# Two subtractions per tile move from VectorE to GpSimd, and six inner tiles change from eight to seven block products

## The chip, the cores and the metric

The kernel runs on one core of a Trainium2 chip. The metric is the device time of one execution in microseconds (us); the times below are those of separate runs, and one further execution was profiled. In the profile PE is TensorE (matmuls), PEld its weight loads, DVE is VectorE, ACT is ScalarE, POOL is GpSimd, SP is SyncE, which here only issues transfers.

## The reference, cut to what matters

A trunk of two layers works on 512 frames of 1024 channels. Each layer has a mixer (layer 0 a recurrent one, layer 1 chunked attention), and behind it a channel mixer, which the change is about:

```
def conv_glu(h, w_in, conv_w, conv_b, w_out):
    gate, val = jnp.split(h @ w_in, 2, axis=-1)          # 1024 -> 2 x 2816
    gp = jnp.pad(gate, ((0, 0), (CONV_W - 1, 0), (0, 0)))
    conv = conv_b + sum(conv_w[j] * gp[:, j:j + seq] for j in range(CONV_W))
    return (jax.nn.gelu(conv, approximate=False) * val) @ w_out
```

The 2816 inner channels are 22 tiles of 128. For each tile a gate and a value are projected from 1024 inputs; the gate is convolved over three frames, goes through a GELU and multiplies the value.

## The kernel before, in words

**Split operands.** TensorE works here in a format with a shorter mantissa than float32 (fp32r). Each operand is therefore split into a high part (a cast, made on ScalarE) and a low part (the number less its high part, a subtraction made on VectorE), and each product is three matmuls: high by high, high by low, low by high. `split_w` (lines 172 and 178) does this for weight tiles of 128x1024, `split_to` (lines 218 and 219) for other operands, the result of each inner tile among them.

**Eights and sevens.** The function `ffn` makes the 22 inner tiles one after the other. A tile called an *eight* (`eight`) is computed plainly: two weight tiles, 2 x 8 x 3 = 48 matmuls on 512 columns. A tile called a *seven* (`seven`) treats gate and value, two halves of the inputs and two halves of the frames as a 2x2 by 2x2 block product and forms it from seven block products in place of eight, as Strassen and Winograd do: 7 x 4 x 3 = 84 matmuls on 256 columns. For this it needs sums and differences of the weight blocks, made by `operands`. Gate weights are loaded into `rg`, and a second transfer, issued by GpSimd (line 442), adds their one half onto the other while it moves. Value weights are loaded into a `wraw` buffer (line 443). VectorE forms one difference in `rg` (line 446) and two in the value tile (lines 448 and 449). Four operands come out: `wv` (the value weights as loaded), `w1`, `wy`, `wx`, each split into high and low. `SEVEN` says which tiles are sevens: of 4 to 20 all but 8, 13 and 18, so 14 sevens and 8 eights in a layer. Tiles 0 to 3 are eights, since sums of the inputs are still made then, and so is 21.

**Order.** The seven's products stand on TensorE's queue as P1 (`wv`), then P6 (`wy`) and P7 (`wx`) of the tile before, and then P2 (`w1`), P3 (`wy`), P4 (`wv`), P5 (`wx`). The result of a tile goes through `gated`: line 397 (ACT), 398 and 399 (DVE), 400 (the GELU, ACT), 401 (the product with the value, DVE), and then its split, a cast on ACT and a subtraction on DVE, into tile j of the inner result (`r1h`/`r1l` or `r2h`/`r2l` for tiles 0 to 7, `f3h`/`f3l` for the others). That low part is read only by the projection back to 1024 channels, behind the last inner tile. In this projection `both` also uses `operands`, three times in layer 0 and twice in layer 1.

**Buffers.** `rg` and `wraw` have two buffers each, `whi` and `wlo` three, `w1` and `wx` one, temporaries six. Each engine works through its queue in order, so an instruction that waits holds up all behind it on that engine; the queues are written in the order that the scheduler gives them at build time.

Of the kernel before, what the change touches and what calls it, by code (L numbers as in the profile page):

```python
# [13 lines left out]
ALU = mybir.AluOpType  # L14
# [98 lines left out]
def trunk_kernel(ctx, tc, A, out):  # L113
    nc = tc.nc
    PE, V, SC, GP = nc.tensor, nc.vector, nc.scalar, nc.gpsimd
# [25 lines left out]
    def Vc(name, i):  # L141
        return vec[:, VOFF[name][0] + i:VOFF[name][0] + i + 1]
# [20 lines left out]
    def tmp(dt=F32, shape=(P, S)):  # L163
        return banks["tmp"].tile(list(shape), dt, name="tmp", tag="tmp")
# [4 lines left out]
    def split_w(raw, n, src=None):  # L169
        hi = wp.tile([P, 1024], F32R, name="whi", tag="whi")  # L170
        lo = wp.tile([P, 1024], F32R, name="wlo", tag="wlo")
        SC.copy(hi[:, :n], raw)  # L172
        if src is not None:

            SC.activation(lo[:, :n], raw, AF.Copy, scale=-1.0)
            GP.dma_start(lo[:, :n], src, accum_op=ALU.add)
        else:
            V.tensor_tensor(lo[:, :n], raw, hi[:, :n], op=ALU.subtract)  # L178
        return hi, lo
# [37 lines left out]
    def split_to(h_, l_, src):  # L217
        SC.copy(h_, src)  # L218
        V.tensor_tensor(l_, src, h_, op=ALU.subtract)  # L219
# [124 lines left out]
            V.tensor_tensor(xT[:, m], xT[:, m], ps[:], op=ALU.add)  # L344
            norm_tile(xT[:, m], m, gain, h_, l_)

    SEVEN = [j for j in range(4, 21) if j % 5 != 3]
    HT = (slice(0, 256), slice(256, 512))

    def ffn(l, hp, ih, il, h_, l_, xT, after, last=None):  # L350
# [5 lines left out]
        def hid(j):  # L356
            return (h_[:, j], l_[:, j]) if j < 8 else (f3h[:, j - 8], f3l[:, j - 8])
# [21 lines left out]
        def sums(k):  # L379
            u, w = tmp(), tmp()  # L380
            for t_, q in ((u, k), (w, k + 4)):
                nc.sync.dma_start(t_[:], xd[q])
                SC.activation(t_[:], t_[:], AF.Copy, scale=Vc(f"ln2_{l}", q))
            four(k, u, w)
# [10 lines left out]
        def gated(j, g, v):  # L395
            c = tmp()
            SC.activation(c[:], g[:], AF.Identity, scale=Vc(f"cw2_{l}", j), bias=Vc(f"cb_{l}", j))
            V.scalar_tensor_tensor(c[:, 1:S], g[:, 0:S - 1], Vc(f"cw1_{l}", j), c[:, 1:S], op0=ALU.mult, op1=ALU.add)
            V.scalar_tensor_tensor(c[:, 2:S], g[:, 0:S - 2], Vc(f"cw0_{l}", j), c[:, 2:S], op0=ALU.mult, op1=ALU.add)
            SC.activation(c[:], c[:], AF.Gelu)  # L400
            V.tensor_tensor(c[:], v, c[:], op=ALU.mult)
            split_to(*hid(j), c[:])

        def eight(j):
            wg = load_w(A["ffn_in"][l, j, 0])
            wv = load_w(A["ffn_in"][l, j, 1])
            pg = ps_f()
            n = 0
            for _ in dense(pg[:], [(wg, K8)], act):
                n += 1  # L410
                if n == 2:
                    yield
            pv = ps_f()
            run(dense(pv[:], [(wv, K8)], act))
            g = tmp()
            V.tensor_tensor(g[:], pg[:], rho[:], op=ALU.mult)
            gated(j, g, pv[:])
# [12 lines left out]
        def own(name, n):  # L430
            return tuple(hp.tile([P, n], F32R, name=name + q, tag=name + q) for q in "hl")

        def split2(w, raw):
            split_to(w[0][:], w[1][:], raw)
            return w

        def operands(src_g, src_v):
            rv = wp.tile([P, 1024], F32, name="wraw", tag="wraw", bufs=2)
            rg = hp.tile([P, 1024], F32, name="rg", tag="rg", bufs=2)
            one, two = slice(0, 512), slice(512, 1024)  # L440
            nc.sync.dma_start(rg[:], src_g)
            GP.dma_start(rg[:, one], src_g[:, two], accum_op=ALU.add)
            nc.sync.dma_start(rv[:], src_v)
            wv = split_w(rv[:], 1024)
            w1 = split2(own("w1", 512), rg[:, one])
            V.tensor_tensor(rg[:, one], rg[:, one], rv[:, one], op=ALU.subtract)
            wy = split_w(rg[:], 1024)
            V.tensor_tensor(rv[:, one], rg[:, two], rg[:, one], op=ALU.subtract)
            V.tensor_tensor(rv[:, two], rv[:, two], rg[:, one], op=ALU.subtract)  # L449
            wx = split2(own("wx", 1024), rv[:])  # L450
            return wv, w1, wy, wx

        def seven(j):
            wv, w1, wy, wx = operands(A["ffn_in"][l, j, 0], A["ffn_in"][l, j, 1])
            b, c = ps_d((P, 256)), ps_f((P, 256))
            v, g = tmp(), tmp()
            prod(b[:], wv, 0, B(0, 0))
            SC.copy(v[:, HT[0]], b[:])
            yield
            prod(c[:], w1, 0, T(1))  # L460
            prod(b[:], wy, 0, T(2), False)
            SC.copy(v[:, HT[1]], b[:])
            a = ps_f((P, 256))
            prod(a[:], wv, 512, B(1, 0))
            V.tensor_tensor(v[:, HT[0]], a[:], v[:, HT[0]], op=ALU.add)
            prod(b[:], wx, 0, T(3), False)
            SC.copy(g[:, HT[1]], b[:])
            V.tensor_tensor(g[:, HT[1]], c[:], g[:, HT[1]], op=ALU.add)
            V.tensor_tensor(g[:, HT[1]], g[:, HT[1]], rho[:, HT[1]], op=ALU.mult)
            yield  # L470
            prod(b[:], wy, 512, T(4), False)
            V.tensor_tensor(g[:, HT[0]], b[:], rho[:, HT[0]], op=ALU.mult)
            prod(c[:], wx, 512, B(1, 1), False)
            V.tensor_tensor(v[:, HT[1]], c[:], v[:, HT[1]], op=ALU.add)
            gated(j, g, v[:])
# [5 lines left out]
        for j in range(NFF):  # L481
            t = (seven if j in SEVEN else eight)(j)
            next(t)
            if rest is not None:
                run(rest)
                rest = None
            if j in SEVEN:
                next(t)
# [3 lines left out]
            if j < 2:  # L492
                sums(2 * j)
                sums(2 * j + 1)
            if j == SEVEN[-1] + 1:
                xT = mid.tile([P, KD, S], F32, name="xT", tag="xT")
# [31 lines left out]
        def both(m):  # L528
            full = [A["ffn_out"][l, m + u] for u in range(2)]
            u0 = pieces(m, ((8, 7), (15, 7)))  # L530
            wv, w1, wy, wx = operands(full[1][:, :1024], full[0][:, :1024])
            yield
            d0 = ps_d()
            run(dense(d0[:], u0, hid))
            b, c = ps_f((P, 256)), ps_f((P, 256))
            s0, s1 = tmp(), tmp()
            prod(b[:], wv, 0, H(0, 0))
            SC.copy(s0[:, HT[0]], b[:])
            prod(c[:], w1, 0, T(1))
            prod(b[:], wy, 0, T(2), False)  # L540
            SC.copy(s0[:, HT[1]], b[:])
            V.tensor_tensor(s0[:, HT[1]], c[:], s0[:, HT[1]], op=ALU.add)
            prod(d0[:, HT[0]], wv, 512, H(1, 0), False)
            prod(b[:], wx, 0, T(3), False)
            SC.copy(s1[:, HT[1]], b[:])
            V.tensor_tensor(s1[:, HT[1]], c[:], s1[:, HT[1]], op=ALU.add)
            prod(b[:], wy, 512, T(4), False)
            SC.copy(s1[:, HT[0]], b[:])
            prod(d0[:, HT[1]], wx, 512, H(1, 1), False)
            u1 = pieces(m + 1, ((8, 7), (15, 7)))  # L550
            yield
            arrive(m, d0, s0)
            d1 = ps_d()
            run(dense(d1[:], u1, hid))
            arrive(m + 1, d1, s1)
# [995 lines left out]
```

## Time and profile before

| | |
|---|---|
| time, median of 3 runs | 1330.07 us (1328.38 to 1333.38) |
| the profiled execution: its time, its span | 1332.23 us, 1330.4 us |
| mean granted TensorE clock | 0.994 |
| busy in the span: PE, DVE, ACT, POOL | 97%, 76%, 54%, 5% |
| inner tiles of layer 0, of layer 1 (about) | 394 to 640 us, 969 to 1215 us |
| the projection behind them, layer 0, layer 1 | 640 to 740 us, 1215 us to the end |

The two stretches of inner tiles are a little over a third of the span. A row of the timeline gives start, duration, engine, line, operation and operands; since an engine begins an instruction while the one before it still writes its last results, the step from start to start is what one instruction takes of a full queue, and the duration is a little longer. In a row of the windows view, busy time and count of instructions stand for each engine in a stretch of time.

### The profile page before, as it was taken

The numbers are of one execution on the slowest core, as the hardware profiler recorded it, in microseconds if no ns is written. First come the engines' busy times: TensorE is split into PE (matmuls) and PEld (weight loads), VectorE is DVE, ScalarE is ACT, GpSimd is POOL, SyncE is SP. The second block draws the span as 40 slices with busy tenths as digits, with TensorE's granted clock in tenths as the row PEclk, the third lists the DMA queues.
The fourth block names the chain that finished last, engine by engine and source line by source line (L and its number), as shares of the span: only waits on it lengthen the run. The fifth ranks groups of instructions, "written<-read, shape, count | busy, mean of one in ns | idle before, by whom it ended". The sixth has DMA issues, their size and how long they took to land.

```text
span 1330.4 us, 24187 instructions
## 1 busy us (share of the span) xinstructions
PE 1293.9 (97%) x9472; PEld 1109.8 (83%) x9472; DVE 1013.8 (76%) x2143; ACT 718.9 (54%) x1236; POOL 67.6 (5%) x110
## 2 busy tenths in 40 slices
PE   7999999999999999999999999999999999999997
PEld 5787777776778999999888878786789999998887
DVE  8886889788468889998756776748678998987644
ACT  6555465555446656655334476657465655553431
POOL 0000000000010000001000000000100000010000
PEclk9998999999999999999999999999999999999999
DMA  5265544554264345355332322222643444453232
GB/s 213 94 178 115 112 101 110 114 127 119 81 205 143 103 128 147 99 135 176 87 108 78 131 88 88 95 95 88 190 166 102 115 126 123 131 167 109 83 87 77
DMA packets 72561, 160.88 MB, mean 121 GB/s; under 512 B 25984, under 2 KB 28288, under 8 KB 72448
## 3 DMA queue, kind: packets, MB, share of 16 engines
q1 hardware_dynamic: 62400, 132.34, 31.8%
q0 software_dynamic: 10048, 27.01, 10.0%
q8 instruction: 74, 1.21, 0.4%
q14 instruction: 39, 0.32, 0.1%
HBM read 148.31 MB, written 11.01 MB: 120 GB/s over the span
## 4 chain that ended last, share of the span: by engine, by line
PE 82%; DVE 10%; ACT 3%; DMA 3%; issue 2%; SPq 0%; DVEq 0%; ACTq 0%; POOLq 0%
PE psd L201 9%; PE psd L202 9%; PE psd L206 9%; PE psd L424 4%; PE psd L427 4%; PE psd L425 4%; PE psf L201 4%; PE psf L202 4%; PE psf L206 4%; PE psf L424 4%; PE psf L427 4%; PE psf L425 4%; DVE Xu L875 2%; DVE Xs L877 1%; PE pss L1328 1%
## 5 line engine op out<-in xcount | busy, mean ns | idle before, releaser
L172 ACT CAST whi<-wraw 128x1024 fp32r<-128x1024 f32 (+1 forms) x169 | 173.6, 1028 | 188.0 <-DMA wraw<-in_ffn_out_dram 44.3
L178 DVE TENSOR_TENSOR wlo<-wraw,whi 128x1024 fp32r<-128x1024 f32 (+1 forms) x150 | 178.8, 1192 | 79.9 <-ACT whi L172 37.7
L201 PE MATMUL psd<-r1h,whi 128*128 128x512 f32 x270 | 109.0, 404 | 0.9 <-DVE xT L344 0.9
L202 PE MATMUL psd<-r1l,whi 128*128 128x512 f32 x270 | 106.9, 396 | 0.0
L201 PE MATMUL psd<-f3h,whi 128*128 128x512 f32 (+1 forms) x238 | 88.8, 377 | 0.0
L202 PE MATMUL psd<-f3l,whi 128*128 128x512 f32 (+1 forms) x238 | 88.7, 377 | 0.0
L206 PE MATMUL psd<-r1h,wlo 128*128 128x512 f32 x270 | 74.1, 405 | 0.0
L201 PE MATMUL psd<-r2h,whi 128*128 128x512 f32 (+1 forms) x168 | 64.6, 389 | 0.8 <-ACT r2h L1335 0.7
L202 PE MATMUL psd<-r2l,whi 128*128 128x512 f32 (+1 forms) x168 | 63.9, 384 | 0.8 <-DVE r2l L219 0.8
L201 PEld LDWEIGHTS psd<-r1h,whi 128*128 128x128 f32 x270 | 50.8, 188 | 12.4 <-issue 1.8
L202 PEld LDWEIGHTS psd<-r1l,whi 128*128 128x128 f32 x270 | 51.0, 189 | 9.7 <-issue 0.3
L206 PEld LDWEIGHTS psd<-r1h,wlo 128*128 128x128 f32 x270 | 49.6, 191 | 10.6 <-issue 0.7
L424 PE MATMUL psd<-xh,whi 128*128 128x256 f32 x224 | 56.3, 284 | 0.0
L206 PE MATMUL psd<-f3h,wlo 128*128 128x512 f32 (+1 forms) x238 | 53.7, 377 | 0.0
L202 PEld LDWEIGHTS psd<-f3l,whi 128*128 128x128 f32 x238 | 44.8, 188 | 8.0
L201 PEld LDWEIGHTS psd<-f3h,whi 128*128 128x128 f32 x238 | 44.8, 188 | 8.0
L201 PE MATMUL psf<-r1h,whi 128*128 128x512 f32 x128 | 50.1, 391 | 0.0
L201 PE MATMUL psf<-r2h,whi 128*128 128x512 f32 x128 | 50.1, 391 | 0.0
L202 PE MATMUL psf<-r2l,whi 128*128 128x512 f32 x128 | 50.0, 390 | 0.0
L202 PE MATMUL psf<-r1l,whi 128*128 128x512 f32 x128 | 49.9, 390 | 0.0
L206 PEld LDWEIGHTS psd<-f3h,wlo 128*128 128x128 f32 x238 | 42.9, 188 | 8.2
L218 ACT CAST wxh<-wraw 128x1024 fp32r<-128x1024 f32 x33 | 34.4, 1044 | 20.2 <-DVE wraw L449 17.5
(538 smaller groups left out, 3757.9 us busy)
## 6 DMA issues: line engine op xcount, KB each, us to landing
wraw<-in_ffn_in_dram SPq DMA_DIRECT2D x60, 512.0 KB, 3.9
rg<-in_ffn_in_dram SPq DMA_DIRECT2D x28, 512.0 KB, 3.5
wraw<-in_ffn_out_dram SPq DMA_DIRECT2D x32, 448.0 KB, 3.4
wraw<-in_wA_dram SPq DMA_DIRECT2D x20, 512.0 KB, 4.0
wraw<-in_w_out_dram SPq DMA_DIRECT2D x16, 512.0 KB, 3.9
wlo<-in_wA_dram POOLq DMA_DIRECT2D x15, 512.0 KB, 7.7
rg<-in_ffn_in_dram POOLq DMA_DIRECT2D x28, 256.0 KB, 5.2
wraw<-in_ffn_out_dram SPq DMA_DIRECT2D x11, 512.0 KB, 3.6
```

Source lines behind the costliest of these rows:

```text
L172: SC.copy(hi[:, :n], raw)
L178: V.tensor_tensor(lo[:, :n], raw, hi[:, :n], op=ALU.subtract)
L201: PE.matmul(ps, wh[:, j * P:(j + 1) * P], ah, start=start and n == 0, stop=False)
L202: PE.matmul(ps, wh[:, j * P:(j + 1) * P], al, start=False, stop=False)
L206: PE.matmul(ps, wl[:, j * P:(j + 1) * P], act(k)[0], start=False, stop=stop and n == len(ks) - 1)
L218: SC.copy(h_, src)
L424: PE.matmul(ps, wh[:, ws], ah, start=start and k == 0, stop=False, skip_group_check=not start)
L425: PE.matmul(ps, wh[:, ws], al, start=False, stop=False, skip_group_check=not start)
L427: PE.matmul(ps, wl[:, o + k * P:o + k * P + P], a(k)[0], start=False, stop=k == 3, skip_group_check=not start)
L875: V.tensor_tensor(uv, L1.rearrange("p i o -> p o i").to_broadcast([P, k, n]), X[:, 0:k, q:q + 1].to_broadcast([P, k, n]), op=ALU.mult)
L877: V.tensor_tensor(X[:, 0:k, q + 1:], X[:, 0:k, q + 1:], uv, op=ALU.add)
L1328: PE.matmul(pso[HS[hh], kt * P:], vS[i // 2][:, kt, (i % 2 * 2 + hh) * 64:(i % 2 * 2 + hh + 1) * 64], pts[hh][:, kt, kt * P:], start=kt == ...
```

## The change

`SEVEN` becomes all tiles from 4 to 20: tiles 8, 13 and 18 of each layer turn from eights into sevens. The low part of every inner tile's result is subtracted on GpSimd, not on VectorE, and so is the second difference in the value tile of `operands`.

```diff
-    SEVEN = [j for j in range(4, 21) if j % 5 != 3]
+    SEVEN = list(range(4, 21))
...
         def gated(j, g, v):
...
             V.tensor_tensor(c[:], v, c[:], op=ALU.mult)
-            split_to(*hid(j), c[:])
+            SC.copy(hid(j)[0], c[:])
+            GP.tensor_tensor(hid(j)[1], c[:], hid(j)[0], op=ALU.subtract)
...
         def operands(src_g, src_v):
...
             V.tensor_tensor(rv[:, one], rg[:, two], rg[:, one], op=ALU.subtract)
-            V.tensor_tensor(rv[:, two], rv[:, two], rg[:, one], op=ALU.subtract)
+            GP.tensor_tensor(rv[:, two], rv[:, two], rg[:, one], op=ALU.subtract)
             wx = split2(own("wx", 1024), rv[:])
```

The changed file has one line more from line 403 on, so lines 442, 446, 448 and 449 are 443, 447, 449 and 450 there. The first place to look at is GpSimd's queue among the inner tiles of layer 0. Before, it holds the adding transfers alone, one for each seven:

```order
L442 DMA rg_5919<-in_ffn_in_dram 128x512
L442 DMA rg_6014<-in_ffn_in_dram 128x512
L442 DMA rg_6143<-in_ffn_in_dram 128x512
L442 DMA rg_6272<-in_ffn_in_dram 128x512
L442 DMA rg_6507<-in_ffn_in_dram 128x512
```

In the changed kernel it reads so (`rg_6200` belongs to tile 11, `rg_6329` to 12, `rg_6458` to 13, `rg_6587` to 14; `tmp_6008`, `tmp_6137`, `tmp_6266` are the results of tiles 8, 9 and 10):

```order
L403 TENSOR_TENSOR f3l_4966<-tmp_6008,f3h_4965 128x512
L443 DMA rg_6329<-in_ffn_in_dram 128x512
L450 TENSOR_TENSOR wraw_6199<-wraw_6199,rg_6200 128x512
L403 TENSOR_TENSOR f3l_4966<-tmp_6137,f3h_4965 128x512
L443 DMA rg_6458<-in_ffn_in_dram 128x512
L450 TENSOR_TENSOR wraw_6328<-wraw_6328,rg_6329 128x512
L403 TENSOR_TENSOR f3l_4966<-tmp_6266,f3h_4965 128x512
L443 DMA rg_6587<-in_ffn_in_dram 128x512
```

So each tile now has the difference for tile n, the low part of the result of tile n-2 and the adding transfer for tile n+2, in this order, on one queue. The second place is VectorE's queue in a tile of the same stretch, from the low part of `w1` to the first instruction behind P6. Before:

```order
L219 TENSOR_TENSOR w1l_6740<-rg_6731,w1h_6739 128x512
L446 TENSOR_TENSOR rg_6731<-rg_6731,wraw_6730 128x512
L401 TENSOR_TENSOR tmp_6668<-tmp_6532,tmp_6668 128x512
L465 TENSOR_TENSOR tmp_6627<-psf_6701,tmp_6627 128x256
L448 TENSOR_TENSOR wraw_6730<-rg_6731 128x512
L178 TENSOR_TENSOR wlo_6745<-rg_6731,whi_6744 128x1024
L219 TENSOR_TENSOR f3l_4966<-tmp_6668,f3h_4965 128x512
L468 TENSOR_TENSOR tmp_6628<-psf_6626,tmp_6628 128x256
L449 TENSOR_TENSOR wraw_6730<-wraw_6730,rg_6731 128x512
L469 TENSOR_TENSOR tmp_6628<-tmp_6628,rho_71 128x256
L472 TENSOR_TENSOR tmp_6628<-psd_6625,rho_71 128x256
```

And in the changed kernel:

```order
L219 TENSOR_TENSOR w1l_6596<-rg_6587,w1h_6595 128x512
L447 TENSOR_TENSOR rg_6587<-rg_6587,wraw_6586 128x512
L401 TENSOR_TENSOR tmp_6524<-tmp_6354,tmp_6524 128x512
L466 TENSOR_TENSOR tmp_6483<-psf_6557,tmp_6483 128x256
L449 TENSOR_TENSOR wraw_6586<-rg_6587 128x512
L178 TENSOR_TENSOR wlo_6601<-rg_6587,whi_6600 128x1024
L469 TENSOR_TENSOR tmp_6484<-psf_6482,tmp_6484 128x256
L470 TENSOR_TENSOR tmp_6484<-tmp_6484,rho_71 128x256
L473 TENSOR_TENSOR tmp_6484<-psd_6481,rho_71 128x256
```

The rows of lines 219 (`f3l`) and 449 are gone from it; the others keep their order.

## The prediction

> **What bounds the kernel now.** I read the page's busy shares first, then the windows view of the two stretches of inner tiles, then the timelines of TensorE and VectorE in one tile.
>
> ```profile
> PE 1293.9 (97%) x9472; PEld 1109.8 (83%) x9472; DVE 1013.8 (76%) x2143; ACT 718.9 (54%) x1236; POOL 67.6 (5%) x110
> 395.00:640.00 245.00, 245.00 (x1639) 226.53 (x1639) 214.53 (x339) 140.48 (x206) 17.05 (x23) 1.00 0.45 132
> 970.00:1215.00 245.00, 245.00 (x1640) 226.69 (x1639) 214.35 (x339) 140.43 (x206) 16.87 (x23) 1.00 0.45 132
> ```
>
> In both stretches (columns: PE, PEld, DVE, ACT, POOL) TensorE has no idle time, 245.00 us of 245, at full granted clock; GpSimd does almost nothing. A modelled busy time can hide gaps, so I look at the steps from start to start.
>
> ```profile
> 433.59 0.39 PE L201 MATMUL psf<-r2h,whi 128*128 128x512 f32 x1
> 437.22 1.98 PE L206 MATMUL psf<-r2h,wlo 128*128 128x512 f32 x8
> 439.03 0.28 PE L424 MATMUL psd<-r2h,whi 128*128 128x256 f32 x1
> ...
> 568.63 0.64 PE L427 MATMUL psd<-xh,wxl 128*128 128x256 f32 x4
> ...
> 578.71 0.64 PE L427 MATMUL psd<-xh,wxl 128*128 128x256 f32 x4
> ```
>
> From 433.59 to 439.03 are the 24 matmuls of half an eight: 5.44 us, 0.227 each. From P5 of one seven to P5 of the next (568.63 to 578.71) are 84 matmuls: 10.08 us, 0.120 each. An eight thus costs 10.88 us, a seven 10.08. These are queue rates without stalls, so TensorE sets the pace here. VectorE is close behind it. This is its whole queue in one seven:
>
> ```profile
> 562.43 0.41 DVE L472 TENSOR_TENSOR tmp<-psd,rho 128x256 f32<-128x256 f32 x1
> 562.77 1.21 DVE L178 TENSOR_TENSOR wlo<-wraw,whi 128x1024 fp32r<-128x1024 f32 x1
> 563.90 0.41 DVE L474 TENSOR_TENSOR tmp<-psf,tmp 128x256 f32<-128x256 f32 x1
> 564.23 0.74 DVE L398 SCALAR_TENSOR_TENSOR tmp<-tmp,vec 128x511 f32<-128x511 f32 x1
> 564.89 1.21 DVE L219 TENSOR_TENSOR wxl<-wraw,wxh 128x1024 fp32r<-128x1024 f32 x1
> 566.03 0.74 DVE L399 SCALAR_TENSOR_TENSOR tmp<-tmp,vec 128x510 f32<-128x510 f32 x1
> 566.69 0.68 DVE L219 TENSOR_TENSOR w1l<-rg,w1h 128x512 fp32r<-128x512 f32 x1
> 567.40 0.69 DVE L446 TENSOR_TENSOR rg<-rg,wraw 128x512 f32<-128x512 f32 x1
> 568.01 0.68 DVE L401 TENSOR_TENSOR tmp<-tmp 128x512 f32<-128x512 f32 x1
> 568.61 0.42 DVE L465 TENSOR_TENSOR tmp<-psf,tmp 128x256 f32<-128x256 f32 x1
> 568.95 0.68 DVE L448 TENSOR_TENSOR wraw<-rg 128x512 f32<-128x512 f32 x1
> 569.54 1.22 DVE L178 TENSOR_TENSOR wlo<-rg,whi 128x1024 fp32r<-128x1024 f32 x1
> 570.68 0.68 DVE L219 TENSOR_TENSOR f3l<-tmp,f3h 128x512 fp32r<-128x512 f32 x1
> 571.28 0.41 DVE L468 TENSOR_TENSOR tmp<-psf,tmp 128x256 f32<-128x256 f32 x1
> 571.62 0.68 DVE L449 TENSOR_TENSOR wraw<-wraw,rg 128x512 f32<-128x512 f32 x1
> 572.22 0.41 DVE L469 TENSOR_TENSOR tmp<-tmp,rho 128x256 f32<-128x256 f32 x1
> 572.55 0.41 DVE L472 TENSOR_TENSOR tmp<-psd,rho 128x256 f32<-128x256 f32 x1
> 562.43:572.55 10.12, 10.12 (x87) 10.12 (x86) 10.09 (x17) 6.60 (x11) 0.87 (x1) 1.00 0.47 130
> ```
>
> From one L472 to the next are 10.12 us, busy for 10.09: among sevens VectorE is as full as TensorE. An eight asks of it only two L178 and five instructions of half that size, by the steps above 2 x 1.14 + 5 x 0.62 = 5.4 us in 10.88, so an eight lets it catch up. It has some lead: `wxl` is written by 566.10 (564.89 + 1.21), and its first matmul starts at 568.63, 2.5 us later.
>
> **The change, part by part.**
>
> *Six tiles from eight to seven.* Six times 10.88 - 10.08 = 0.80 us on TensorE: **-4.8 us**, if nothing else holds it up. On VectorE each adds 10.1 - 5.4 = 4.7 us, before the next part.
>
> *Two subtractions leave VectorE.* The step from L219 (`f3l`) to L468 is 0.60 us, from L449 to L469 0.60. A seven then asks 10.1 - 1.2 = **8.9 us** of VectorE in 10.08. This by itself saves nothing on TensorE, which is the bound; it pays for the eights that are gone.
>
> *The same two on GpSimd.* No row of before shows GpSimd reading a tile. The nearest ones:
>
> ```profile
> L677 POOL MEMSET acc<- 128x512 f32 x1 | 0.5, 531 | 20.4 <-DVE rha L253 20.4
> L442 POOL DMA_DIRECT2D rg<-in_ffn_in_dram x28 | 24.4, 872 | 348.8 <-DVE wlo L178 117.1 <-DVE wxl L219 57.7 <-DVE tmp L474 54.4
> rg<-in_ffn_in_dram SPq DMA_DIRECT2D x28, 512.0 KB, 3.5
> rg<-in_ffn_in_dram POOLq DMA_DIRECT2D x28, 256.0 KB, 5.2
> 569.13 0.61 ACT L218 CAST f3h<-tmp 128x512 fp32r<-128x512 f32 x1
> 573.19 1.05 ACT L218 CAST wxh<-wraw 128x1024 fp32r<-128x1024 f32 x1 [0.44 <-PE psf L425]
> 574.87 0.60 ACT L218 CAST w1h<-rg 128x512 fp32r<-128x512 f32 x1
> ```
>
> GpSimd writes one 128x512 stream in 0.53 us; a subtraction has three streams, so 1.6 us at the upper end; at the lower, VectorE's 0.68. I take 1.2, between them and nearer the GpSimd row. With the adding transfer's 0.87 that is 3.3 us of GpSimd per tile (at the upper end 4.1) of 10.08: the queue has room.
>
> The Trainium skill, "GPSIMD Engine Reference", section 3.1, gives 4497 ns for a two-input addition of 2048 elements per partition; a quarter of it, an estimate of 1.1 us, would leave the sum as it is.
>
> *What is queued behind them.* The second difference for tile n now starts after L448, which ends at 569.63, and ends near 570.9 (at 1.6 us: 571.3), where VectorE's L449 ended at 572.30; the cast that reads it starts at 573.19. So that operand is earlier, not later. The low part of tile n-2's result can start when its cast ends (569.74), stands behind that difference, and ends near 572.1 to 572.9; it is read only after the last inner tile. The adding transfer stands behind both. Its buffer is free at 570.9, the first transfer takes 3.5 us (574.4), so the low part does not hold it up; issue 0.9 and landing 5.2 give 580.5. The `w1` cast at 574.87 is that of tile n+1; the one for n+2, which this transfer feeds, comes a tile later, near 584.9: some 4 us to spare. The last two low parts of a layer stand behind eight transfers that rebuild the residual stream, but are read 20 of 22 tile steps into the next projection, at 0.45 us per tile step 9 us later. All of this costs **0**; it stops being free when a GpSimd subtraction takes over 3 us.
>
> *What GpSimd costs VectorE.* This is the open term. If the two engines did not disturb each other, VectorE would be at 8.9 of 10.08. If a VectorE instruction with both inputs in SBUF stood still while GpSimd works, it would lose up to 1.6 us per subtraction. In the queue above only L465, L468, L472 and L474 read a matmul result; they take 4 x 0.33 = 1.3 of 10.1 us, so 85% of what is left is exposed. I take half speed while both run: 1.2 x 0.85 x 0.5 = 0.5 us per subtraction, 1.0 per tile, so 9.9 of 10.08 us: still below TensorE. The half is a choice between no and full blocking; no row decides it. The point at which it matters can be worked out. VectorE may lose 10.08 - 8.9 = 1.2 us per tile without falling behind, and its lead of 2.5 us spread over 17 sevens adds 0.15. So the threshold is **0.67 us per subtraction**, almost what each took from VectorE (0.60).
>
> The Trainium skill, "SBUF — State Buffer", section "Who interferes with whom", speaks against this part: a VectorE instruction with two SBUF inputs contends with a GpSimd instruction that reads SBUF, and it calls the shared pair of ports an exclusive lock. No trace here shows it yet, since GpSimd reads nothing in before; if it holds as a lock, the first rival below is the outcome.
>
> *The sum.* The profiled execution took 1332.23 us (span 1330.4 and 1.8 around it), less 4.8 is 1327.4. Its time was 2.16 us above the median of the three runs, so against the median: 1330.07 - 4.8 = **1325.3 us**, -0.36%.
>
> **Rivals.**
>
> 1. *VectorE becomes the bound.* GpSimd's subtraction stops VectorE's two-input instructions for its whole length: 1.2 x 0.85 = 1.0 us each, 2.0 per tile, 10.9 of 10.08 us. Per layer 17 x 0.85 - 2.5 (lead) = 12 us, for both 24, less 4.8: **1349 us**. For it: VectorE has nothing to spare among sevens, and the eights that let it catch up are gone. Against it: GpSimd's two come close together near the end of VectorE's round, where VectorE waits for P6 if it is early, so part of the blocking falls into its 1.2 us of new idle time. With a third of it hidden so, 8.9 + 1.4 = 10.3 of 10.08: 17 x 0.2 - 2.5 = 1 us per layer, about 1327 again. It decides from 0.67 us per subtraction on.
>
> 2. *GpSimd's queue delays an operand.* If a subtraction takes over 3 us in company, the adding transfer lands after the `w1` cast wants it; 0.4 us late in each of the 34 tiles would be +13.6 - 4.8: **1339 us**. For it: three kinds of work that wait for three engines share one queue in order. Against it: the 4 us to spare, and a queue that is filled to a third (3.3 of 10.08 us) as priced.
>
> 3. *It is better than the sum.* VectorE now gets ahead of TensorE, and waits of a tenth of a microsecond outside the steady tiles go. The steps above show hardly any stall that could go, so at most 2 us: **1323 us**.
>
> 4. *The change does not do what it says.* The three tiles per layer are sevens in TensorE's queue; only if their step were not 0.120 us would the 4.8 us fail to appear. That would be **1330 us**; nothing speaks for it, as the rate is that of 14 sevens per layer.
>
> **How the numbers follow.** Under half a per cent (6.65 us) is what a measurement of this kernel can hardly tell from no change; even the whole 4.8 us lies inside it. Forecast 56%, rival 1 27% (a fifth of this near the lower end of its price, within half a per cent), rival 2 6%, rival 3 8%, rival 4 3%. Faster needs under 1323.4: half of rival 3, and 5% for the spread of runs, 9%. Slower needs over 1336.7: four fifths of rival 1, rival 2, and 2% for stalls that I have not seen, 30%. The rest, 61%, is within. The forecast's own range is 1322 to 1330, by the spread of the three runs. The range is 1322 to 1346: it leaves out the upper half of rival 1.
>
> **What would show it.** Right: P5 to P5 stays at 10.08 us through all 17 sevens; the windows view of the inner tiles, each stretch 2.4 us shorter, has TensorE full, VectorE at 9 to 10 us per seven, and its 128x1024 subtractions under 2.0 us; the GpSimd subtractions at about 1.2 us. Wrong: rows of L178 or L219 far longer than 1.22 us beside GpSimd's; TensorE idle with `wxl` or `wlo` as the releaser; P5 to P5 near 10.9 us. If VectorE's steps are unchanged beside a busy GpSimd, the sharing that I assume does not exist, and the same time would be right for another reason.

## The result, and the profile after

The changed kernel takes **1351.03 us** in the median of 4 runs (1349.36 to 1352.35). The kernel before, run beside it, takes 1329.44 us (1328.38 to 1333.38). The ratio is **1.0154**, with an interval of 1.0134 to 1.0173: slower by some 21 us. The profiled execution took 1349.75 us, with a span of 1348.0 us at a mean granted clock of 0.996. The forecast of 1325.3 us was wrong, and the range of 1322 to 1346 does not hold the result.

These are the page's busy shares of the changed kernel and, below them, the shares of its chain of work that ended last:

```profile
PE 1295.0 (96%) x9688; PEld 1117.1 (83%) x9688; DVE 1064.8 (79%) x2114; ACT 733.8 (54%) x1266; POOL 212.6 (16%) x199
PE 64%; DVE 26%; ACT 4%; issue 4%; DMA 2%; SPq 0%; DVEq 0%; ACTq 0%
```

VectorE has fewer instructions than before (2114 against 2143) and yet is busy for 51 us more (1064.8 against 1013.8), and its share of the chain is 26%, where it was 10%. TensorE's busy time hardly changed. Where the time went is shown by the windows view of the two stretches of inner tiles and of one seven (columns: stretch; its length; busy time of PE, PEld, DVE, ACT, POOL; granted clock; DMA share; GB/s), and by the waits of TensorE over the whole span:

```profile
395.00:640.00 245.00, 235.54 (x1696) 221.82 (x1695) 231.96 (x316) 144.76 (x217) 85.21 (x64) 1.00 0.48 131
562.40:572.50 10.10, 9.50 (x80) 9.30 (x79) 10.03 (x14) 6.13 (x10) 3.86 (x3) 1.00 0.46 116
970.00:1215.00 245.00, 235.77 (x1703) 222.12 (x1702) 229.90 (x310) 144.16 (x216) 82.34 (x65) 1.00 0.47 130
...
PE psf L425 <- DVE tmp L469: 18.4, 30, 0.8
```

TensorE, full before, is now idle for 9.5 and 9.2 us in the two stretches, while VectorE is full (10.03 of 10.10 us in one seven). TensorE waits 30 times, in 34 sevens, at the same place: its first matmul of P7 waits for VectorE's L469. In the changed file, lines from 403 on have numbers one higher than before, so this is L468 of before. Four rows of TensorE's timeline give the length of one seven, from P5 to P5, and the stall in it:

```profile
562.73 0.64 PE L428 MATMUL psd<-xh,wxl 128*128 128x256 f32 x4
...
565.61 0.64 PE L428 MATMUL psd<-xh,wlo 128*128 128x256 f32 x4
566.85 0.38 PE L425 MATMUL psf<-r2h,wxh 128*128 128x256 f32 x1 [0.60 <-DVE tmp L469]
...
573.67 0.64 PE L428 MATMUL psd<-xh,wxl 128*128 128x256 f32 x4
```

From 562.73 to 573.67 are 10.94 us, where the kernel before needed 10.08: 0.86 us more in a seven, and 30 stalls make 26 us. The wait's own 0.60 is smaller than that because the end of the matmul before the gap is modelled: the row at 565.61 is four matmuls at 0.12, so the next should have started at 566.09, and started 0.76 us later; the other 0.1 us is lost right behind it.

VectorE's queue for the same seven, and the two GpSimd instructions that run beside it, say why L469 is late:

```profile
561.82 0.69 DVE L401 TENSOR_TENSOR tmp<-tmp 128x512 f32<-128x512 f32 x1
562.42 0.42 DVE L466 TENSOR_TENSOR tmp<-psf,tmp 128x256 f32<-128x256 f32 x1
562.76 1.47 DVE L449 TENSOR_TENSOR wraw<-rg 128x512 f32<-128x512 f32 x1
564.15 2.32 DVE L178 TENSOR_TENSOR wlo<-rg,whi 128x1024 fp32r<-128x1024 f32 x1
566.38 0.41 DVE L469 TENSOR_TENSOR tmp<-psf,tmp 128x256 f32<-128x256 f32 x1
566.83 0.43 DVE L470 TENSOR_TENSOR tmp<-tmp,rho 128x256 f32<-128x256 f32 x1
```

```profile
562.05 1.62 POOL L450 TENSOR_TENSOR wraw<-wraw,rg 128x512 f32<-128x512 f32 x1 [1.31 <-ACT tmp L400]
563.64 1.74 POOL L403 TENSOR_TENSOR f3l<-tmp,f3h 128x512 fp32r<-128x512 f32 x1
```

Two VectorE rows have grown, and no others: L449 from 0.68 to 1.47 (+0.79) and L178 from 1.22 to 2.32 (+1.10), **1.89 us** together. The two engines can be read as taking turns:

- GpSimd's L450 is issued at 562.05 while VectorE works on L401. It gets its turn when VectorE goes on to L466 at 562.42, and ends at 563.67, 1.25 us later.
- L466 has one input in PSUM (`psf`; the tiles that matmuls write are called `ps...` and lie in PSUM, all others that an engine works on lie in SBUF), and passes GpSimd at its usual 0.42. L449 has both inputs in SBUF. It is issued at 562.76, and ends at 564.23: 0.6 us, which is its usual work, behind GpSimd's end.
- GpSimd's L403, issued at 563.64, gets its turn when VectorE is done with L449 (its next instruction begins at 564.15), and ends at 565.38, 1.23 us later.
- L178, issued at 564.15, ends at 566.47: 1.1 us, again its usual work, behind that.

VectorE's round was 10.1 us. Less 1.2 for the two subtractions that left it, plus 1.89, plus 0.1 (L470 needs the result of L469, and now stands directly behind it: 0.45 us from start to start in place of 0.33) it is 10.9 us, which is what P5 to P5 shows. That this is how all sevens go is seen in the groups by line, VectorE's for the first stretch and GpSimd's for the whole span (count, busy time, mean in ns of one; then idle time ahead of them):

```profile
L178 DVE TENSOR_TENSOR wlo<-rg,whi 128x1024 fp32r<-128x1024 f32 x17 | 37.7, 2218 | 0.1
L449 DVE TENSOR_TENSOR wraw<-rg 128x512 f32<-128x512 f32 x17 | 24.0, 1413 | 0.0
```

```profile
L450 POOL TENSOR_TENSOR wraw<-wraw,rg 128x512 f32<-128x512 f32 x39 | 62.1, 1591 | 188.0 <-DVE wlo L178 140.7 <-ACT tmp L400 39.3 <-PE psf L428 6.7
L403 POOL TENSOR_TENSOR f3l<-tmp,f3h 128x512 fp32r<-128x512 f32 x28 | 52.4, 1873 | 18.7 <-ACT f3h L402 18.7
```

The mean of all 17 rows of L178 is 2.22 us, and of L449 1.41. GpSimd's means of 1.59 and 1.87 hold its own waiting too.

### The profile page after: what moved, and what is told of

It reads as the page before. It is cut to its first block, busy times and chain, and to the rows that moved or that the text cites. A ratio compares the mean times of both kernels' runs of the same rounds, so it can differ in the third digit from the quotient of the medians.

```text
span 1348.0 us, 24889 instructions
## 1 busy us (share of the span) xinstructions
PE 1295.0 (96%) x9688; PEld 1117.1 (83%) x9688; DVE 1064.8 (79%) x2114; ACT 733.8 (54%) x1266; POOL 212.6 (16%) x199
## 3 DMA queue, kind: packets, MB, share of 16 engines
q8 instruction: 76, 1.25, 0.4%
## 4 chain that ended last, share of the span: by engine, by line
PE 64%; DVE 26%; ACT 4%; issue 4%; DMA 2%; SPq 0%; DVEq 0%; ACTq 0%
PE psd L201 10%; PE psd L202 10%; PE psd L206 9%; DVE wlo L178 6%; PE psf L425 4%; PE psf L428 3%; PE psf L426 3%; DVE wraw L449 3%; PE psf L201 2%; PE psf L202 2%; DVE tmp L399 2%; PE psf L206 2%; DVE rg L447 2%; DVE tmp L401 1%; DVE w1l L219 1%
## 5 line engine op out<-in xcount | busy, mean ns | idle before, releaser
L178 DVE TENSOR_TENSOR wlo<-wraw,whi 128x1024 fp32r<-128x1024 f32 (+1 forms) x144 | 171.5, 1191 | 66.1 <-PE psd L206 35.2
L450 POOL TENSOR_TENSOR wraw<-wraw,rg 128x512 f32<-128x512 f32 x39 | 62.1, 1591 | 188.0 <-DVE wlo L178 140.7
L178 DVE TENSOR_TENSOR wlo<-rg,whi 128x1024 fp32r<-128x1024 f32 x39 | 81.6, 2091 | 4.3 <-PE psd L206 4.1
L425 PE MATMUL psd<-xh,whi 128*128 128x256 f32 x272 | 68.3, 283 | 0.3 <-ACT tmp L459 0.3
L443 POOL DMA_DIRECT2D rg<-in_ffn_in_dram x34 | 30.1, 887 | 168.3 <-DMA rg<-in_ffn_in_dram 136.3
L449 DVE TENSOR_TENSOR wraw<-rg 128x512 f32<-128x512 f32 x39 | 55.9, 1432 | 0.1
L403 POOL TENSOR_TENSOR f3l<-tmp,f3h 128x512 fp32r<-128x512 f32 x28 | 52.4, 1873 | 18.7 <-ACT f3h L402 18.7
L425 PEld LDWEIGHTS psd<-xh,whi 128*128 128x128 f32 x272 | 52.2, 192 | 0.6 <-ACT tmp L459 0.5
L172 ACT CAST whi<-rg 128x1024 fp32r<-128x1024 f32 x39 | 41.0, 1052 | 20.5 <-PE psf L428 15.7
L426 PE MATMUL psd<-tl,whi 128*128 128x256 f32 x204 | 51.9, 283 | 0.0
```

Source lines behind the costliest of these rows:

```text
L403: GP.tensor_tensor(hid(j)[1], c[:], hid(j)[0], op=ALU.subtract)
L425: PE.matmul(ps, wh[:, ws], ah, start=start and k == 0, stop=False, skip_group_check=not start)
L426: PE.matmul(ps, wh[:, ws], al, start=False, stop=False, skip_group_check=not start)
L450: GP.tensor_tensor(rv[:, two], rv[:, two], rg[:, one], op=ALU.subtract)
```

## The experiments

Three theories stood against each other, and the expectations speak of them. **The lock (A)**, which is rival 1: while GpSimd reads SBUF, a VectorE instruction with two SBUF inputs waits until it has finished, and the other way round. **Sharing (B)**, the forecast's assumption: both go on, VectorE at a part of its speed. **Place (C)**: a subtraction costs nothing or everything, by what stands next to it in the queues, so that one of the two carries the whole loss.

All kernels differ by the lines shown, from before or from the changed kernel, or from another version where the text says so. The stretch in the table runs from the first matmul of the first inner tile to the first matmul of the projection. What follows a stretch takes the same time in all of them, to within some tenths of a microsecond. The part ahead of the first inner tile varies from run to run by itself, between 388 and 394 us, which is why a median may differ from the stretches by one or two microseconds.

| kernel | ratio to before, interval | layer 0 / layer 1 stretch, us |
|---|---|---|
| before | 1 | 230.2 / 230.0 |
| the change | 1.0154 [1.0134, 1.0173] | 241.0 / 240.4 |
| 17 sevens, both subtractions on VectorE | 0.9951 [0.9936, 0.9966] | 227.6 / 227.5 |
| 14 sevens, both on GpSimd | 1.0105 [1.0089, 1.0121] | 237.6 / 237.0 |
| 17 sevens, low part on GpSimd | 0.9989 [0.9975, 1.0003] | 231.1 / 230.0 |
| 17 sevens, weight difference on GpSimd | 1.0042 [1.0027, 1.0056] | 234.0 / 233.8 |
| 17 sevens, low part on GpSimd, made twice | 1.0240 [1.0217, 1.0264] | 247.7 / 247.7 |
| the change, GpSimd only writes | 0.9928 [0.9904, 0.9952] | 227.4 / 227.3 |
| the change, GpSimd reads one input | 0.9926 [0.9897, 0.9955] | 227.4 / 227.3 |
| 17 sevens, low part of `wv` by transfer | 1.0139 [1.0105, 1.0172] | 239.9 / 238.0 |
| sevens 2 to 20, VectorE | 1.0025 [1.0009, 1.0042] | 232.6 / 232.5 |
| sevens 3 to 20, VectorE | 0.9940 [0.9924, 0.9955] | 227.9 / 227.9 |

**The six tiles alone.** Against before:

```diff
-    SEVEN = [j for j in range(4, 21) if j % 5 != 3]
+    SEVEN = list(range(4, 21))
```

> The list of sevens is 4 to 20, both subtractions stay on VectorE. All theories: VectorE is asked for 10.1 us per seven against 10.08 on TensorE, 17 x 0.02 us is less than its lead of 2.5 us, so the 4.8 us appear in full: 1325 us (ratio 0.996), P5 to P5 at 10.08 us. If instead the eights were needed for VectorE to catch up (waits for P6 and for casts that the sum of steps does not show), 0.2 us or more per seven: 1328 to 1332 us.

1323.48 us against 1329.99 for before beside it. The stretches are 2.6 and 2.5 us shorter, three times 0.80 in each and 0.1 to 0.2 more. The windows view shows TensorE full with 17 sevens, and VectorE busy for 229.77 of 245 us:

```profile
395.00:640.00 245.00, 245.00 (x1755) 232.21 (x1754) 229.77 (x366) 149.23 (x225) 19.11 (x25) 1.00 0.49 135
```

So the term of -4.8 us is right, and VectorE could take the three further sevens without any help. Run again beside the later versions, the same kernel was to show whether that holds:

> The same kernel as sevens_only, on the chip of sevens_3_20, to compare the two: 0.995 to 0.997 of the kernel before.

It took 1322.51 us, ratio 0.9939 [0.9924, 0.9955], a little better than expected. No version that computes the same result was faster, and it is faster than both kernels of the case.

**The two subtractions alone.** The changed kernel with the old list:

```diff
-    SEVEN = list(range(4, 21))
+    SEVEN = [j for j in range(4, 21) if j % 5 != 3]
```

> Both subtractions on GpSimd, the old list with 14 sevens and 8 eights. Theory A (lock: a GpSimd instruction that reads SBUF shuts out every VectorE instruction with two SBUF inputs for its whole length, some 1.2 us): each seven lags 0.8 us, four in a row 3.4 us, less a lead of 2.5, and the eight between lets VectorE catch up: 4 to 8 us in all, 1334 to 1338 us. Theory B (sharing: both engines run slower but neither stands still, and the loss of the changed kernel is mostly where it fell): VectorE at 9.9 us, no stall: 1330 us.

1343.26 us, so the move alone loses 13.3 us in the median; the two stretches are 7.4 and 7.0 us longer. TensorE's waits in layer 0 (400 to 740 us) stand at the same place:

```profile
PE psf L425 <- DVE tmp L469: 4.8, 7, 0.9
```

The loss was larger than expected. The expectation gave TensorE's operands a lead to use up; at this place there is hardly one (see the points below), and only the eights give some back.

**One subtraction each.** The changed kernel with one of the two back on VectorE, so that only the low part is on GpSimd:

```diff
-            GP.tensor_tensor(rv[:, two], rv[:, two], rg[:, one], op=ALU.subtract)
+            V.tensor_tensor(rv[:, two], rv[:, two], rg[:, one], op=ALU.subtract)
```

> 17 sevens, only the low part of the results on GpSimd, the weight difference on VectorE. Theory A: VectorE 10.1 - 0.6 + 1.05 = 10.5 us per seven, 17 x 0.45 - 2.5 = 5 us per layer, less 4.8: 1335 us, and one VectorE instruction per tile longer by about 1 us. Theory C (the stall comes from one instruction's place: L469, which frees P7's bank in PSUM, stands behind two long instructions; VectorE's total is not the point): the loss does not follow the total; with L469 behind the weight difference and one 1024-wide subtraction it is either that of the changed kernel (1350 us) or none (1325 us).

and with only the weight difference on GpSimd:

```diff
-            SC.copy(hid(j)[0], c[:])
-            GP.tensor_tensor(hid(j)[1], c[:], hid(j)[0], op=ALU.subtract)
+            split_to(*hid(j), c[:])
```

> 17 sevens, only the weight difference on GpSimd, the low part on VectorE. Theory A: the same 10.5 us per seven, 1335 us; with low_only the two losses over 1325 us add up to about that of the changed kernel, less the lead counted twice (2 x 5 us): 10 + 10 + 5 = 25 us. Theory B with half speed: 10.0 us, 1325 us. Theory C: as for low_only, all or nothing.

1328.01 and 1335.15 us. Both lose against the 17 sevens on VectorE (3.5 and 2.5 us per layer, 6.4 and 6.3), so neither is free, and neither carries all of the change's 13.4 and 12.9: place (C) falls. The 1335 us that theory A gave for each came out for the weight difference, but not for the low part: there VectorE's loss was taken at 1.05 us, and the rows below show 0.78. The timelines with only the low part on GpSimd, VectorE's first and then GpSimd's, say the most about lock or sharing (L469, L450 and L470 are L468, L449 and L469 of before):

```profile
558.16 1.22 DVE L178 TENSOR_TENSOR wlo<-rg,whi 128x1024 fp32r<-128x1024 f32 x1
559.30 0.42 DVE L469 TENSOR_TENSOR tmp<-psf,tmp 128x256 f32<-128x256 f32 x1
559.63 1.46 DVE L450 TENSOR_TENSOR wraw<-wraw,rg 128x512 f32<-128x512 f32 x1
561.01 0.41 DVE L470 TENSOR_TENSOR tmp<-tmp,rho 128x256 f32<-128x256 f32 x1
...
571.32 0.41 DVE L470 TENSOR_TENSOR tmp<-tmp,rho 128x256 f32<-128x256 f32 x1
```

```profile
558.46 2.08 POOL L403 TENSOR_TENSOR f3l<-tmp,f3h 128x512 fp32r<-128x512 f32 x1 [2.73 <-ACT f3h L402]
```

GpSimd's subtraction is issued 0.3 us into L178. L178 keeps its 1.22 us, though a GpSimd row stands beside it for 0.8 of them; under sharing (B) it would be longer. GpSimd's own row is 2.08 long, and ends at 560.54, 1.24 us after L178 has made way. L450, which comes next with two SBUF inputs, takes 1.46 where it took 0.68. Whoever is first goes through whole, and the other waits: the lock (A). The two instructions that meet have no tile in common (`f3l`, `tmp` and `f3h` here, `wraw` and `rg` there), so it is no wait for a result. From L470 to L470 are 10.31 us.

With only the weight difference on GpSimd, the group of L448 and the step from one L398 to the next show the same size:

```profile
L448 DVE TENSOR_TENSOR wraw<-rg 128x512 f32<-128x512 f32 x17 | 24.4, 1436 | 0.0
```

```profile
555.52 0.74 DVE L398 SCALAR_TENSOR_TENSOR tmp<-tmp,vec 128x511 f32<-128x511 f32 x1
565.96 0.74 DVE L398 SCALAR_TENSOR_TENSOR tmp<-tmp,vec 128x511 f32<-128x511 f32 x1
```

L448 goes from 0.68 to 1.44, and VectorE's round is 10.44 us. Per layer, (10.31 - 10.08) x 17 is 3.9 us and (10.44 - 10.08) x 17 is 6.1, beside measured losses of 3.5 and 2.5, and of 6.4 and 6.3. For the change, (10.94 - 10.08) x 17 is 14.6 against 13.4 and 12.9 measured, since the first sevens of a layer don't stall in full. In each case one subtraction takes 0.6 us off VectorE's round and puts about 0.8 back; with the weight difference on GpSimd another 0.1 is lost, as in the change, because L469 stands directly behind L468.

**GpSimd only writes.** The changed kernel with writes of zeros in place of the two subtractions:

```diff
-            GP.tensor_tensor(hid(j)[1], c[:], hid(j)[0], op=ALU.subtract)
+            GP.memset(hid(j)[1].bitcast(F32), 0.0)
...
-            GP.tensor_tensor(rv[:, two], rv[:, two], rg[:, one], op=ALU.subtract)
+            GP.memset(rv[:, two], 0.0)
```

> The changed kernel with both GpSimd subtractions replaced by a GpSimd memset of the same 128x512 output: it reads nothing; the low parts of the inner results and the second weight difference are left out (zeros in their place). Theory A (the lock is on reading): no VectorE instruction gets longer (0.68 and 1.22 us stay), VectorE at 8.9 us per seven, TensorE at 10.08: as sevens_only, 1323 us. If writing locks as well: L449 and the 128x1024 subtraction behind it get up to 0.5 us longer each, 9.9 us, 1323 to 1326 us; the rows tell, not the time.

This kernel leaves both subtractions out. 1322.47 us against 1329.64, no stall, and no row of VectorE that is longer. Its group of L449 for the first stretch, one write of GpSimd, a VectorE instruction with two SBUF inputs that starts inside it, and the windows view:

```profile
L449 DVE TENSOR_TENSOR wraw<-rg 128x512 f32<-128x512 f32 x17 | 11.6, 683 | 0.0
...
557.99 0.52 POOL L450 MEMSET wraw<- 128x512 f32 x1 [8.31 <-DVE wlo L178]
...
558.13 0.74 DVE L398 SCALAR_TENSOR_TENSOR tmp<-tmp,vec 128x511 f32<-128x511 f32 x1
...
395.00:640.00 245.00, 245.00 (x1756) 232.18 (x1755) 210.75 (x329) 151.62 (x226) 28.53 (x43) 1.00 0.47 136
```

L449 is back at 0.68, and L398 takes its usual 0.74 beside the write. In the changed kernel the same L398 once met a GpSimd instruction that reads, at the end of the inner tiles of layer 0 (GpSimd's row first):

```profile
628.59 1.31 POOL L403 TENSOR_TENSOR f3l<-tmp,f3h 128x512 fp32r<-128x512 f32 x1 [1.52 <-ACT f3h L402]
```

```profile
628.66 1.78 DVE L398 SCALAR_TENSOR_TENSOR tmp<-tmp,vec 128x511 f32<-128x511 f32 x1
```

There it took 1.78, and ended 0.54 us behind GpSimd's end (630.44 and 629.90). So it is GpSimd's reading that stops VectorE. The evidence is the 17 writes into the value tile of each layer; those for the low parts wait for nothing and mostly ran ahead of time. VectorE's instructions stand in the same order in this kernel's sevens as in those of the changed one, so that order, which differs from that of the 17 sevens on VectorE, is not what costs the time. VectorE is freed here of both subtractions, and the stretches are only 0.2 us shorter than with the 17 sevens alone: freeing VectorE was worth next to nothing.

**GpSimd reads one input.** Copies in place of the subtractions, so that GpSimd reads one stream and not two:

```diff
-            GP.tensor_tensor(hid(j)[1], c[:], hid(j)[0], op=ALU.subtract)
+            GP.tensor_copy(hid(j)[1], c[:])
...
-            GP.tensor_tensor(rv[:, two], rv[:, two], rg[:, one], op=ALU.subtract)
+            GP.tensor_copy(rv[:, two], rg[:, one])
```

> The changed kernel with both GpSimd subtractions replaced by a GpSimd copy of one input to the same output: one stream read, the subtrahend left out. Theory A: the lock lasts as long as the copy, 0.5 to 0.8 us by the memset's 0.53; the VectorE instruction beside it gets longer by up to that, 0.3 to 0.6 us each, VectorE at 9.5 to 10.1 us per seven: 1323 to 1327 us. If only two reading streams collide: no row longer, 1323 us.

1322.23 us, no stall. The rows, VectorE's and then GpSimd's:

```profile
563.33 0.77 DVE L449 TENSOR_TENSOR wraw<-rg 128x512 f32<-128x512 f32 x1
564.02 1.63 DVE L178 TENSOR_TENSOR wlo<-rg,whi 128x1024 fp32r<-128x1024 f32 x1
```

```profile
562.60 0.96 POOL L450 COPY wraw<-rg 128x512 f32<-128x512 f32 x1 [2.10 <-ACT tmp L400]
563.50 1.07 POOL L403 CAST f3l<-tmp 128x512 fp32r<-128x512 f32 x1
```

VectorE still waits, but for less: +0.09 and +0.41, 0.5 per seven in place of 1.89. By the same taking of turns L403 begins its work when L178 begins (564.02) and ends at 564.57, 0.55 us later, and L178 ends 1.08 us behind that. One reading stream is enough to stop it; a shorter GpSimd instruction stops it for less time, and VectorE then stays below TensorE's 10.08.

**The same subtraction twice.** The kernel with only the low part on GpSimd, its line written a second time:

```diff
             GP.tensor_tensor(hid(j)[1], c[:], hid(j)[0], op=ALU.subtract)
+            GP.tensor_tensor(hid(j)[1], c[:], hid(j)[0], op=ALU.subtract)
```

> low_only with GpSimd's subtraction made twice on the same tile, one behind the other, the same result. Theory A (lock, first come first served, some 1.2 us each): the second one is taken when VectorE's next two-input instruction ends and holds up the one behind it, so VectorE loses another 0.8 to 1.2 us per seven: 11.1 to 11.5 us instead of 10.30, the inner tiles of a layer 14 to 20 us longer than in low_only, in all 1357 to 1368 us. Sharing without a lock: the same total reading spread over more of VectorE's instructions, each a little longer.

1363.32 us against 1331.77. Line numbers from 404 on are two above those of before, so L451 is L449 and L471 is L469:

```profile
557.65 0.42 DVE L470 TENSOR_TENSOR tmp<-psf,tmp 128x256 f32<-128x256 f32 x1
557.99 1.44 DVE L451 TENSOR_TENSOR wraw<-wraw,rg 128x512 f32<-128x512 f32 x1
559.35 1.51 DVE L471 TENSOR_TENSOR tmp<-tmp,rho 128x256 f32<-128x256 f32 x1
...
569.37 1.45 DVE L451 TENSOR_TENSOR wraw<-wraw,rg 128x512 f32<-128x512 f32 x1
```

```profile
556.81 2.07 POOL L403 TENSOR_TENSOR f3l<-tmp,f3h 128x512 fp32r<-128x512 f32 x1 [3.86 <-ACT f3h L402]
558.96 1.62 POOL L404 TENSOR_TENSOR f3l<-tmp,f3h 128x512 fp32r<-128x512 f32 x1
```

The round is now 11.38 us (557.99 to 569.37), 1.07 more than with one. The second subtraction hits an instruction of 256 columns, which grows from 0.41 to 1.51: the price is set by GpSimd's instruction, not by the length of the one that it stops. GpSimd's rows end 1.23 us after VectorE's L470 begins (557.65 to 558.88) and 1.23 us after its L471 is issued behind L451 (559.35 to 560.58). The rows differ by 0.45 us in length, but the work is the same 1.23.

This also gives the rule for the price. A VectorE instruction issued at the moment GpSimd gets its turn waits about 1.1 us (L178 in the change, L471 here). Where an instruction that reads PSUM comes between, its 0.33 us pass meanwhile, and the next one waits 0.75 to 0.8 (L449 in the change, L450 with one low part, L451 here). In the change L178 has no such instruction ahead of it, so the two subtractions together cost more than the sum of each alone.

**Another way to relieve VectorE.** The 17 sevens with the low part of `wv` made by ScalarE and an adding transfer, as the kernel does elsewhere, so that no SBUF tile is read by GpSimd (against the 17 sevens on VectorE):

```diff
-            wv = split_w(rv[:], 1024)
+            wv = split_w(rv[:], 1024, src_v)
```

> 17 sevens, both subtractions on VectorE; the low part of wv (1.14 us of VectorE per tile) is made as the mixers make theirs: ACT writes the negative high part, a GpSimd transfer adds the weights from memory. VectorE 10.1 - 1.1 = 9.0 us per seven, but no lock, since the transfer's descriptors read no tile through that port. TensorE is the bound already in sevens_only, so no gain over it: 1323 us if the transfer (7.7 us to land in the mixers) is early enough; else TensorE waits for wlo by up to 3 us per tile: 1330 to 1420 us.

1350.2 us, as slow as the change, for another reason. The waits of TensorE in layer 0, the landing time of that transfer, and the windows view of the stretch:

```profile
PE psd L427 <- DMA wlo<-in_ffn_in_dram: 8.6, 8, 2.8
...
wlo<-in_ffn_in_dram POOLq DMA_DIRECT2D x34, 512.0 KB, 6.1
...
395.00:640.00 245.00, 236.36 (x1701) 223.88 (x1700) 204.39 (x339) 160.74 (x236) 33.61 (x42) 0.99 0.67 167
```

VectorE is relieved (204.39 us busy), but the transfers now take 0.67 of the DMA engines in place of 0.49, and TensorE waits for `wlo`: 8.6 of the 12.3 us by which this stretch is longer than with the 17 sevens alone.

**More sevens.** The 17 sevens on VectorE, with tiles 2 and 3, and then tile 3 alone, added:

```diff
-    SEVEN = list(range(4, 21))
+    SEVEN = list(range(2, 21))
```

> Subtractions on VectorE, tiles 2 to 20 sevens: two more per layer than sevens_only. TensorE: 4 x 0.80 = 3.2 us less, 1320 us (ratio 0.993), if the sums of the inputs, which VectorE makes beside tiles 0 to 3, are ready; they ask some 4 x 3.5 us of VectorE there, so tiles 2 and 3 may wait: up to 10 us per layer, 1340 us.

```diff
-    SEVEN = list(range(4, 21))
+    SEVEN = list(range(3, 21))
```

> Subtractions on VectorE, tiles 3 to 20 sevens. One tile per layer more than sevens_only, 2 x 0.80 = 1.6 us less on TensorE: 1322 us. In sevens_2_20 tile 2 waited for the sums of the inputs (2.8 us at once) and for VectorE behind them; tile 3 starts 10.9 us later, which should cover most of it. If not, 3 us per layer more than sevens_only: 1329 us.

1333.21 us (before, run beside it, 1329.64), and 1324.01 (1331.77). Row one is the longest wait of TensorE in the first seven with tile 2, row two the one with tile 3 alone:

```profile
420.71 0.58 PE L424 MATMUL psd<-xh,whi 128*128 128x256 f32 x1 [2.51 <-ACT tmp L458]
```

```profile
429.02 0.38 PE L424 MATMUL psd<-xh,whi 128*128 128x256 f32 x1 [0.85 <-ACT tmp L458]
```

The first seven starts before its operands are there. With tile 2 this costs a wait of 2.5 us, and then half the clock for some 4 us. With tile 3 the wait of 0.85 takes the 0.80 that the further seven gains: 227.9 us per stretch, against 227.6.

## Why the prediction was wrong, point by point

**TensorE's -4.8 us** was right: 17 sevens with everything on VectorE made the two stretches 5.1 us shorter. **GpSimd's price** was right too: 1.2 us was taken, and 1.23 to 1.25 is what each takes once it has its turn. The queue behind it cost **0** as said: no operand waited for an adding transfer in the stretches, and GpSimd's idle time in the groups above is waiting for other engines. One place in that part was misread: the second weight difference was to start behind VectorE's first one (L448 of before), but it doesn't wait for it. It is issued 0.7 us ahead of it (562.05 and 562.76), and so is what L449 runs into. **VectorE's 1.2 us** did leave its queue.

**The step that failed** is "I take half speed while both run: 1.2 x 0.85 x 0.5 = 0.5 us per subtraction, 1.0 per tile", from which 9.9 us per seven followed for VectorE, below TensorE's 10.08. The runs showed 0.79 and 1.10, 1.89 per tile, and 10.9 us per seven. The prediction named both ends, no blocking and full blocking, and took the middle, with no row to decide; the middle is not what happens. In these rows an instruction either waits for the other engine's end or isn't touched. The argument that made rival 1 look smaller, that part of the blocking falls into VectorE's new idle time ahead of P6, had it backwards: once 1.89 is added for 1.2 taken, there is no idle time (10.03 of 10.10 busy). A move that saves 0.60 per instruction and costs 0.75 to 1.1 can't pay on an engine that is full.

**The Trainium skill**, "SBUF — State Buffer", section "Who interferes with whom", was weighed in the prediction and not followed. The rows agree with it in the three statements that bear on this case: an exclusive lock (L178 at 1.22 and GpSimd at 2.08 side by side), nothing for a VectorE instruction with one SBUF input (L466 at 0.42), nothing when GpSimd only writes (L398 at 0.74).

**The lead of 2.5 us** was measured at the wrong instruction. It was read at `wxl`, VectorE's result for P5. But VectorE's L468 of before also holds TensorE: it reads the PSUM tile `c`, to which P7's matmuls then add. It ended at 571.69 (571.28 + 0.41), and before's P7 starts at

```profile
571.99 0.28 PE L424 MATMUL psf<-r2h,wxh 128*128 128x256 f32 x1
```

so the margin was 0.3 us, not 2.5. The **threshold** of 0.67 us per subtraction, worked out with 0.15 for that lead, is really about 0.6, what each takes off VectorE. One sign under "What would show it" came out otherwise for the same reason: the releaser is L469's `tmp`, not `wxl` or `wlo`, while the long L178 and the 10.9 us from P5 to P5 came as written there.

**Rival 1** had the mechanism, the place and nearly the price: 2.0 per tile (1.89), 10.9 per round (10.94), 1349 us (1351.0). Its lead of 2.5 us per layer, which wasn't there, is partly offset by the sevens at the start of a layer that don't stall, so that 1349 came so close is in part luck. The range left its upper half out, and that was the half that came. Rivals 2 and 4 saw nothing of theirs happen. Rival 3's 1323 us came about in the version without GpSimd, but there by the part ahead of the inner tiles, which varies, and not by waits that went.

**What stays open.** The rows are as a lock would give them, to within 0.1 us. Whether the hardware hands the access to SBUF over per instruction, or in pieces that are long beside these instructions, no run here shows.

## What to carry to other kernels

Before work is moved from a full VectorE to GpSimd, count the VectorE instructions with two SBUF inputs that will stand beside it: here each GpSimd subtraction of 128x512 saved VectorE 0.6 us and cost it 0.75 to 1.1, and the whole move cost some 27 us against the same kernel without it (1351.0 against 1323.5). When a change has two parts of which one is to pay for the other, run the other alone: here VectorE's full queue had been enough. And measure a lead at every instruction that TensorE waits for, the readers of a PSUM tile that it is about to add to among them, not only at the operands.

## What the runs showed of the hardware

- GpSimd's row includes its waiting: 1.62 to 2.08 us for 1.23 us of work. A GpSimd duration beside a busy VectorE says little of the operation's price.
- Copies with one input stop VectorE as well, for +0.09 and +0.41 us; writes of zeros do not.
- A short VectorE instruction pays as much as a long one: 256 columns grew from 0.41 to 1.51 us.
- In the two places below, after a wait of TensorE of 2.5 to 2.8 us, the granted clock was 0.50 for 3.3 to 4 us. The windows view shows it behind the wait for the transfer (first row, the kernel with the low part of `wv` by transfer) and behind the wait of tile 2 (second row, sevens 2 to 20); the granted clock is the third number from the end:

```profile
447.90:451.20 3.30, 3.30 (x18) 3.30 (x17) 0.42 (x1) 2.06 (x3) 1.18 (x2) 0.50 0.32 53
```

```profile
421.00:425.00 4.00, 4.00 (x19) 3.87 (x19) 3.04 (x7) 1.85 (x3) 0.00 (x0) 0.50 0.00 0
```

By an estimate, half of 3.3 to 4 us, these two waits cost another 1.6 to 2 us behind themselves; what sets off the lower clock, no run here shows. The 0.6 us waits of the changed kernel did not do it: its clock stayed at 1.00 in both stretches.
